# Sums of weight blocks formed at other places, and copies out of PSUM banks at a higher priority, in a one-layer encoder kernel

## The chip, the cores and the metric

The kernel runs on one core of a Trainium2 chip. The metric is device time in microseconds (us) of one execution. Three runs of the kernel before took 856.43 to 857.36 us, with a median of 857.22 us.

## The reference

One encoder layer works on 512 tokens of width 1024, in float32:

```
x += W_out [ HGRN2_group(n) ; mLSTM_group(n) ],  n = RMSNorm(x)
x += CrossAttn(RMSNorm(x), RMSNorm(mem))          (4 heads, 256 memory tokens, output matrix w_xo 1024x1024)
x += relu(RMSNorm(x) @ w_up)^2 @ w_down           (w_up 1024x4096, w_down 4096x1024)
out = RMSNorm(x)
```

The change touches what happens from the last matrix product of the cross-attention (w_xo) through the squared-ReLU part (w_up, w_down), and the order in which some transfers are issued ahead of that.

## The kernel before, in words

**Products.** TensorE multiplies float32 as two halves. ACT writes the high half of a tile (`wh`, or `xT`, `yT`, `a` for activations), VectorE (DVE) subtracts it from the source and so gets the low half (`wl`); both stand in line 325 (`split_out`). Three matmuls (high x high, high x low, low x high) then make one product. A weight block is 512 KB: it is loaded into one of three `st` buffers by SyncE (SP), split into one of three `wh` and one of three `wl` buffers, and used.

**Stream.** Up to the cross-attention's query matrix, weights come through `weights()`, which splits a few blocks ahead and loads one more (line 245). In the same call `next_form()` may do one step on sums of blocks that are needed much later.

**Seven products.** w_xo and the squared-ReLU part are cut in 2x2 blocks and computed with seven products instead of eight, named P1 to P7, each for two halves a and b (in the code g = 0, 1) of the inner dimension or of the columns. P1, P2 and P3 use plain blocks. P5, P7, P6 and P4 use sums of blocks: P7 is two blocks, P6 is P7 plus a third, P4 is P6 plus the fourth, P5 is two. The sums are never formed by an engine: a transfer puts the first block at its place, and a transfer issued by GpSimd (POOL) that adds to what stands there brings the next one. The squared-ReLU part runs as eight stages: stage 0, 2, 4, 6 are up products (one quarter of the 4096 columns each, TensorE lines 1551 to 1553) and stage 1, 3, 5, 7 are the down products of the same quarter (lines 1279 to 1281).

- The sums for the up stages, and P7 of the down stages, are made in HBM (tiles `form_<stage>_P<n>_<g>`, written by lines 282 and 298) by a fixed list of 80 steps, from which `next_form()` takes one at a time: a start (SP copies a block), an add (POOL), or a copy of a finished sum to be built on (SP, line 298).
- The sums P5, P6 and P4 of the down stages are made in SBUF, in the two buffers `msum` (tile name `as`): `sum_base` loads the first term (SP, line 282 for P5 and line 1223 for P6, which starts from the P7 in HBM), `sum_add` adds (POOL, line 282).
- The sums for w_xo are made in SBUF by `add_block` (POOL, line 1163): `U` for P5 (in an `as` buffer) and `T3` for P7, P6 and P4 in turn (tile `gate`). T3 is split for P7, then a block is added, it is split for P6, a block is added, it is split for P4.

**Order.** From w_xo on, TensorE's order is the order in which the code is written. On the other engines a scheduler orders instructions by the order of the code and by priority (`tc.high_priority()` moves an instruction ahead), and `behind(a, b)` pins a behind b on the same engine. SP and POOL issue their transfers in that order too: an issue that has to wait holds back all issues behind it on its queue. `mahead(n)` splits the weights of jobs n to n+2 of the squared-ReLU part, at high priority, and loads those of n+3 to n+6; the list `due` holds sum steps that are to be done when a job is split.

**The norm ahead of the squared-ReLU part.** While w_xo's last products are added to the residual (line 1363), `rstd_half` computes the scale of 256 tokens at a time; its last operation is a power on POOL (line 1412), one for each half of the tokens. TensorE turns the result (line 1428), ACT copies it (line 1430), and DVE multiplies the activations by it (line 1417). The residual itself is turned by TensorE (line 1389) and copied out by ACT (line 1396).

**Banks in an up stage.** P1, P6, P7 and P4 of one half accumulate in the same PSUM bank, and so do P5 and P3. After P1, P5 and P6 ACT copies the bank's present value out (lines 1557, 1564, 1567), and after P2 and P7 DVE adds it (lines 1559, 1575); the next product in that bank may start only then. In a down stage DVE adds each bank to the residual (line 1482).

Of the kernel before, what the change touches and what calls it, by code (L numbers as in the profile page):

```python
# [13 lines left out]
AF = mybir.ActivationFunctionType  # L14
ALU = mybir.AluOpType
# [3 lines left out]
P = 128  # L19
# [61 lines left out]
def trunk(ctx: ExitStack, tc: tile.TileContext, x, mem, wpk, vec, cst, lmask, rmask, rows, out):  # L81
    nc = tc.nc
# [50 lines left out]
    nh = misc[:, 0:1]  # L133
# [8 lines left out]
    def behind(a, b):  # L142

        tc.add_manual_dep(a.ins, b.ins.name, mybir.DependencyInfo(mybir.DependencyClass.NoSync, mybir.DependencyReason.DATA),
                          reason="order of an engine")
# [113 lines left out]
    def weights(key):  # L259
        i = SIDX[key]  # L260
        with (tc.high_priority() if i > 2 else ExitStack()):
            for n in range(i, i + 3):
                split(n)
            load(i + 3)
        if i >= 6 and (i < 46 or i % 3):
            next_form()
        return hl_tiles[i]

# [9 lines left out]
    def mfill(eng, dst, st, g, b, accumulate=False):  # L278
        kw = dict(accum_op=ALU.add) if accumulate else {}
        if st % 2 == 0:  # L280
            dst = dst.rearrange("p (n c) -> p n c", n=2)
        return eng.dma_start(out=dst, in_=mblock(st, g, *b), max_dma_last_dim=4096, **kw)  # L282
# [877 lines left out]

    def add_block(dst, idx, accumulate=True):
        kw = dict(accum_op=ALU.add) if accumulate else {}
        return gp.dma_start(out=dst, in_=wpk[idx], **kw)

    PLAIN = {"P1": (0, 0), "P2": (1, 0), "P3": (1, 1)}
    SUMS = {"P6": "T3", "P5": "U", "P7": "T3", "P4": "T3"}
# [50 lines left out]
    def sum_base(st, p, g):  # L1217
        t = msum[p != "P5"][:, g * 1024:g * 1024 + 1024]
        if p == "P5":
            mfill(nc.sync, t, st, g, (0, 1))  # L1220
        else:
            assert (st, "P7", g) in formed
            nc.sync.dma_start(out=t, in_=mforms[st, "P7", g][:, :], max_dma_last_dim=4096)

    def sum_add(st, p, g):
        mfill(gp, msum[p != "P5"][:, g * 1024:g * 1024 + 1024], st, g, (1, 0) if p == "P4" else (0, 0), True)

    def msplit(n):
        if n >= len(MJ):
# [18 lines left out]
    def mahead(n):  # L1248
        with tc.high_priority():
            for m in range(n, n + 3):  # L1250
                msplit(m)
            for m in range(n + 3, n + 7):
                mload(m)
        if n % 2:
            next_form()
        return mhl[n]

# [6 lines left out]
    def by_blocks(st, sta, banks, done, ready=None, after=None):  # L1264

        mlp = st >= 0
        user = {"P1": 0, "P2": 1, "P5": 2, "P6": 0, "P3": 2, "P7": 0 if mlp else 3, "P4": 0}
        opens = {"P1", "P2", "P5"} if mlp else {"P1", "P2", "P5", "P7"}
        jobs = MORDER[st] if mlp else JOBS
        held = {}  # L1270

        def product(p, g, u, w, first, end):
            for k in range(2):
                ah, al = [t[:, u * P:u * P + P] for t in sta[2 * g + k][p]]
                bh, bl = [t[:, k * 512:k * 512 + 512] for t in w]
                new = first and k == 0 and p in opens
                fl = dict(skip_group_check=True)
                ps = held[user[p]][u]
                pe.matmul(ps, lhsT=ah, rhs=bh, start=new, stop=False, **fl)  # L1279
                pe.matmul(ps, lhsT=ah, rhs=bl, start=False, stop=False, **fl)  # L1280
                pe.matmul(ps, lhsT=al, rhs=bh, start=False, stop=end and k == 1, **fl)  # L1281
            if after is not None:
                after()

        def ahead(n):
            if mlp:
                return mahead(len(JOBS) * st + n)
            with tc.high_priority():
                for m in range(n, n + 3):
                    job(m)  # L1290
                i = max(hl_tiles)
                for m in range(i + 1, i + 4):
                    load(m)
                for m in range(n + 3 - len(JOBS), n + 7 - len(JOBS)):
                    if m >= 0:
                        mload(m)
            return job(n)

        def finished(p, u):
            for t0, c, sign in INTO[mlp][p]:  # L1300
                done(t0 + u, c, held[user[p]][u], sign, (p, t0, c) in LAST[mlp])

        n = 0
        while n < len(jobs):
            p, g = jobs[n]
            if ready is not None:
                ready(p, g)
            if user[p] not in held:
                held[user[p]] = banks[user[p]]()
            if p == "P4":  # L1310
                ws = [ahead(n), ahead(n + 1)]
                for u in range(2):
                    for g in range(2):
                        product(p, g, u, ws[g], False, g == 1)
                    finished(p, u)
                n += 2
                continue
            w = ahead(n)
            for u in range(2):
                product(p, g, u, w, g == 0, g == 1)  # L1320
                if g == 1:
                    finished(p, u)
            n += 1
# [80 lines left out]
    def rstd_half(u):  # L1404

        s2_, m2_ = tiny(2), tiny(2)
        a = ap(st2, 4 * u, [2, 2], [1, 1])
        b = ap(st2, 4 * u + 1, [2, 2], [1, 1])
        v.tensor_tensor(out=s2_[:, :].unsqueeze(2), in0=a, in1=b, op=ALU.add)
        v.tensor_scalar(out=m2_, in0=s2_, scalar1=1.0 / D, scalar2=EPS, op0=ALU.mult, op1=ALU.add)  # L1410
        rt[u] = tiny(2)
        gp.tensor_tensor(out=rt[u], in0=m2_, in1=nh.to_broadcast([P, 2]), op=ALU.pow)

    def times_r(x, u, h):
        z = x[:, h * 512:h * 512 + 512]
# [42 lines left out]
        xf[p] = [YT1()[:, :], YT1()[:, :]]  # L1458
    rrow = RG()
    by_blocks(-1, sta_o, (mm2, mm2, sm2, sm2), add_out, heads_in, after_product)  # L1460
    msum.extend([A16(), A16()])
    for fn in (sum_base, sum_add):
        for q in ("P5", "P6"):
            for g in range(2):
                fn(1, q, g)


    def finish(t, r, first):
# [10 lines left out]

    def add_to(t, c, ps, sign, fin=False):  # L1480
        z = xr[t, c]
        added = v.tensor_tensor(out=z, in0=z, in1=ps, op=ALU.add if sign > 0 else ALU.subtract)  # L1482
        if not fin:
            return
        squared = stats(st3, t, c)
# [18 lines left out]
    def up(st):  # L1504
# [30 lines left out]
        for n, (p, g) in enumerate(MORDER[st]):  # L1535
# [18 lines left out]
                after_product()  # L1554
            if p == "P1":
                y[0, g] = msum[g][:, 2048:2560]
                sc.activation(y[0, g], ps, AF.Copy)
            elif p == "P2":
                v.tensor_tensor(out=y[0, g], in0=y[0, g], in1=ps, op=ALU.add)
                square(y[0, g], y[0, g])  # L1560
                form("P1", g, y[0, g], yt)
            elif p == "P5":
                y[3, g] = T2()[:, 0:512]
                sc.activation(y[3, g], ps, AF.Copy)
            elif p == "P6":
                y[1, g] = rrow[:, (1 - g) * 512:(1 - g) * 512 + 512]
                sc.activation(y[1, g], ps, AF.Copy)  # L1567
            if p in ("P3", "P6") and {("P3", g), ("P6", g)} <= set(MORDER[st][:n + 1]):
                z = y[1, g]
                v.tensor_tensor(out=z, in0=C[g], in1=z, op=ALU.subtract)  # L1570
# [132 lines left out]
```

## Time and profile before

| | us |
|---|---|
| median of three runs | 857.22 |
| profiled execution | 855.08 |
| its span (first to last instruction) | 853.2 |
| TensorE (PE) busy | 812.7 (95%) |
| VectorE (DVE) busy | 620.8 (73%) |
| ScalarE (ACT) busy | 487.3 (57%) |
| GpSimd (POOL) busy | 92.7 (11%) |

In the rows below, times count from the start of the span. A row of the timeline has the start, the duration, the engine, the line, the operation and its tiles; in brackets stands how long the engine had been idle before it and what ended that. A row of windows has the stretch and its length, the busy time and the number of instructions of each engine, then the clock granted to TensorE (1.00 is full), the busy share of the 16 DMA engines and the GB/s.

### The profile page before, as it was taken

The page shows a single profiled execution, that of the slowest core. Times are in us where ns is not written, and L with a number is a line of the kernel's source. Part 1 is how long each engine was busy: PE and PEld are TensorE (multiplying, and loading weights), DVE is VectorE, ACT ScalarE, POOL GpSimd, SP SyncE. Part 2 cuts the span into 40 slices and gives each one's busy share as a digit, 9 for nine tenths or more (in the row PEclk, how much of TensorE's full clock was granted, in tenths as well). Part 3 has the DMA queues.
Part 4 walks back from the last instruction along what each step waited for, and adds up shares of the span by engine and source line. Part 5 has one row for each costly group of instructions (what it writes and reads, how often), then busy time and mean ns, then how long its engine had stood idle before and what let it go on. Part 6 is the DMA issues. An engine that isn't in the chain of part 4 may idle for free.

```text
span 853.2 us, 14086 instructions
## 1 busy us (share of the span) xinstructions
PE 812.7 (95%) x5438; PEld 700.4 (82%) x5438; DVE 620.8 (73%) x1033; ACT 487.3 (57%) x854; POOL 92.7 (11%) x132
## 2 busy tenths in 40 slices
PE   8999999999999999999999867899899999999995
PEld 6787888877889888888888757888898799889984
DVE  6568875897589887545578577797479658865885
ACT  5247465436585575444555474763577358537854
POOL 2002000220111200100201112010202000100001
PEclk9999999999999999999999988999999999999998
DMA  7377734494469586744826939679989975876552
GB/s 270 112 243 182 219 130 148 103 233 144 150 152 263 147 279 225 188 157 129 201 67 151 238 82 265 187 191 340 260 276 244 287 222 193 205 226 215 172 148 99
DMA packets 56021, 165.16 MB, mean 194 GB/s; under 512 B 5329, under 2 KB 5457, under 8 KB 55954
## 3 DMA queue, kind: packets, MB, share of 16 engines
q1 hardware_dynamic: 40624, 123.94, 41.7%
q0 software_dynamic: 15040, 39.85, 25.4%
q8 instruction: 43, 0.70, 0.3%
q10 hardware_dynamic: 290, 0.47, 0.2%
q14 instruction: 24, 0.20, 0.1%
HBM read 162.14 MB, written 44.04 MB: 242 GB/s over the span
## 4 chain that ended last, share of the span: by engine, by line
PE 55%; DVE 13%; DMA 12%; issue 9%; ACT 8%; POOL 1%; POOLq 0%; ACTq 0%; SPq 0%; DVEq 0%
PE mm L328 9%; PE mm L330 9%; PE mm L329 9%; DMA st<-in_wpk 6%; DVE wl L325 6%; ACT wh L325 5%; PE sm L1281 3%; PE sm L1280 3%; PE sm L1279 3%; DMA st<-form_P 3%; PE sm L1551 2%; PE sm L1552 2%; PE sm L1553 2%; DMA gate<-in_wpk 2%; PE mm L1552 1%
## 5 line engine op out<-in xcount | busy, mean ns | idle before, releaser
L325 ACT ACTIVATE wh<-st 128x1024 fp32r<-128x1024 f32 x163 | 172.3, 1059 | 188.0 <-PE mm L329 43.6
L325 DVE TENSOR_TENSOR wl<-st,wh 128x1024 fp32r<-128x1024 f32 x163 | 199.0, 1223 | 109.5 <-ACT wh L325 108.1
L328 PE MATMUL mm<-xT,wh 128*128 128x512 f32 x288 | 115.5, 402 | 0.0
L330 PE MATMUL mm<-xT,wl 128*128 128x512 f32 x288 | 113.1, 393 | 0.1
L329 PE MATMUL mm<-xT,wh 128*128 128x512 f32 x288 | 112.7, 391 | 0.3 <-DVE xT L1042 0.3
L1279 PE MATMUL sm<-wh,a 128*128 128x512 f32 x180 | 70.3, 390 | 1.2 <-DVE vv L1482 1.2
L1281 PE MATMUL sm<-wh,a 128*128 128x512 f32 x180 | 70.3, 391 | 0.9 <-DVE a L325 0.9
L1280 PE MATMUL sm<-wl,a 128*128 128x512 f32 x180 | 70.3, 391 | 0.5 <-DVE wl L325 0.5
L330 PEld LDWEIGHTS mm<-xT,wl 128*128 128x128 f32 x288 | 54.1, 188 | 11.7 <-DVE wl L325 0.3
L329 PEld LDWEIGHTS mm<-xT,wh 128*128 128x128 f32 x288 | 54.2, 188 | 10.9 <-DVE xT L1042 0.9
L328 PEld LDWEIGHTS mm<-xT,wh 128*128 128x128 f32 x288 | 54.1, 188 | 10.8 <-ACT wh L325 0.3
L282 POOL DMA_DIRECT2D form_P<-in_wpk x40 | 42.7, 1508 | 68.9 <-DMA form_P<-form_P 53.1
L282 POOL DMA_DIRECT2D as<-in_wpk x24 | 21.2, 894 | 240.9 <-DMA as<-in_wpk 97.4
L1551 PE MATMUL sm<-yT,wh 128*128 128x256 f32 x128 | 38.5, 301 | 6.6 <-ACT rg L1567 6.6
L1281 PEld LDWEIGHTS sm<-wh,a 128*128 128x128 f32 x180 | 33.8, 188 | 8.6 <-DVE a L325 1.6
L1279 PEld LDWEIGHTS sm<-wh,a 128*128 128x128 f32 x180 | 33.8, 188 | 8.5 <-ACT wh L325 1.6
L1280 PEld LDWEIGHTS sm<-wl,a 128*128 128x128 f32 x180 | 33.8, 188 | 8.3 <-DVE wl L325 1.4
L325 ACT ACTIVATE wh<-as 128x1024 fp32r<-128x1024 f32 x26 | 27.5, 1056 | 19.3 <-PE sm L1281 13.3
L1552 PE MATMUL sm<-yT,wh 128*128 128x256 f32 x128 | 38.0, 297 | 0.0
L1553 PE MATMUL sm<-yT,wl 128*128 128x256 f32 x128 | 37.9, 296 | 0.0
L1552 PE MATMUL sm<-xT,wh 128*128 128x256 f32 x128 | 36.3, 284 | 1.0 <-DVE xT L325 1.0
L1553 PE MATMUL mm<-xT,wl 128*128 128x256 f32 x128 | 36.3, 284 | 0.7 <-DVE wl L325 0.7
(388 smaller groups left out, 2134.7 us busy)
## 6 DMA issues: line engine op xcount, KB each, us to landing
st<-in_wpk SPq DMA_DIRECT2D x123, 512.0 KB, 4.2
form_P<-in_wpk POOLq DMA_DIRECT2D x40, 512.0 KB, 10.2
st<-form_P SPq DMA_DIRECT2D x40, 512.0 KB, 6.2
as<-in_wpk POOLq DMA_DIRECT2D x28, 512.0 KB, 8.3
form_P<-in_wpk SPq DMA_DIRECT2D x24, 512.0 KB, 6.2
form_P<-form_P SPq DMA_DIRECT2D x16, 512.0 KB, 5.9
gate<-in_wpk POOLq DMA_DIRECT2D x8, 512.0 KB, 6.1
as<-in_wpk SPq DMA_DIRECT2D x8, 512.0 KB, 3.6
```

What stands on the lines that cost most here:

```text
L282: return eng.dma_start(out=dst, in_=mblock(st, g, *b), max_dma_last_dim=4096, **kw)
L325: return sc.activation(dst_hi, src, AF.Copy), v.tensor_tensor(out=dst_lo, in0=src, in1=dst_hi.bitcast(F32), op=ALU.subtract)
L328: pe.matmul(ps, lhsT=ah, rhs=bh, start=first, stop=False)
L329: pe.matmul(ps, lhsT=ah, rhs=bl, start=False, stop=False)
L330: pe.matmul(ps, lhsT=al, rhs=bh, start=False, stop=last)
L1279: pe.matmul(ps, lhsT=ah, rhs=bh, start=new, stop=False, **fl)
L1280: pe.matmul(ps, lhsT=ah, rhs=bl, start=False, stop=False, **fl)
L1281: pe.matmul(ps, lhsT=al, rhs=bh, start=False, stop=end and k == 1, **fl)
L1551: pe.matmul(o, lhsT=hi[:, z], rhs=xh[:, m], start=new, stop=False, **fl)
L1552: pe.matmul(o, lhsT=hi[:, z], rhs=xl[:, m], start=False, stop=False, **fl)
L1553: pe.matmul(o, lhsT=lo[:, z], rhs=xh[:, m], start=False, stop=kt == 3, **fl)
```

## The change

```diff
@@ weights(key)
-        if i >= 6 and (i < 46 or i % 3):
+        if i >= 6:
             next_form()
@@ add_block
-        return gp.dma_start(out=dst, in_=wpk[idx], **kw)
+        pool_add[0] = gp.dma_start(out=dst, in_=wpk[idx], **kw)
@@ sum_base(st, p, g)
         if p == "P5":
-            mfill(nc.sync, t, st, g, (0, 1))
+            o = mfill(nc.sync, t, st, g, (0, 1))
         else:
-            nc.sync.dma_start(out=t, in_=mforms[st, "P7", g][:, :], max_dma_last_dim=4096)
+            o = nc.sync.dma_start(out=t, in_=mforms[st, "P7", g][:, :], max_dma_last_dim=4096)
+        behind(o, last_load[0])
@@ sum_add(st, p, g)
-        mfill(gp, msum[p != "P5"][:, g * 1024:g * 1024 + 1024], st, g, (1, 0) if p == "P4" else (0, 0), True)
+        o = mfill(gp, msum[p != "P5"][:, g * 1024:g * 1024 + 1024], st, g, (1, 0) if p == "P4" else (0, 0), True)
+        behind(o, last_made[0] if st > 1 or p != "P5" else pool_add[0])
@@ mahead(n)
-        if n % 2:
+        if n % 2 and n >= len(JOBS):
             next_form()
@@ by_blocks, ahead(n)  (w_xo)
+            if n == 4:
+                msum.append(A16())
+                for g in range(2):
+                    sum_base(1, "P5", g)
             return job(n)
@@ rstd_half
-        gp.tensor_tensor(out=rt[u], in0=m2_, in1=nh.to_broadcast([P, 2]), op=ALU.pow)
+        pool_add[0] = gp.tensor_tensor(out=rt[u], in0=m2_, in1=nh.to_broadcast([P, 2]), op=ALU.pow)
@@ behind w_xo
-    msum.extend([A16(), A16()])
-    for fn in (sum_base, sum_add):
-        for q in ("P5", "P6"):
-            for g in range(2):
-                fn(1, q, g)
+    msum.append(A16())
+    due.extend((2 + g, sum_add, 1, "P5", g) for g in range(2))
+    due.extend((3 + 2 * g, sum_base, 1, "P6", g) for g in range(2))
+    due.extend((7 + 2 * g, sum_add, 1, "P6", g) for g in range(2))
@@ add_to (down stages)
-        added = v.tensor_tensor(out=z, in0=z, in1=ps, op=ALU.add if sign > 0 else ALU.subtract)
+        with tc.high_priority():
+            added = v.tensor_tensor(out=z, in0=z, in1=ps, op=ALU.add if sign > 0 else ALU.subtract)
@@ up(st): the copies behind P1, P5 and P6 (ACT) and the add behind P2 (DVE), each in the same way
-                sc.activation(y[1, g], ps, AF.Copy)
+                with tc.high_priority():
+                    sc.activation(y[1, g], ps, AF.Copy)
```

TensorE's order is the same in both kernels. Below, the rows of the other engines' orders are given at three places; the second number in a tile's name counts tiles and differs between the kernels without meaning.

**POOL, from w_xo's last sums to the first down stage.** `gate` is T3, `as` are the sums of the first down stage, the two TENSOR_TENSOR are the norm's powers, `form` are the sums in HBM. Before:

```order
L1163 DMA gate_631_4282<-in_wpk 128x1024
L282 DMA as_791_5101<-in_wpk 128x1024 x2
L1163 DMA gate_630_4281<-in_wpk 128x1024
L282 DMA as_792_5102<-in_wpk 128x1024 x2
L1163 DMA gate_631_4282<-in_wpk 128x1024
L1412 TENSOR_TENSOR tiny_773_5014<-tiny_772_5011,misc_75 128x2
L1412 TENSOR_TENSOR tiny_790_5099<-tiny_789_5096,misc_75 128x2
L282 DMA form_6_P7_1_3344<-in_wpk 256x1x512
L282 DMA form_4_P5_0_3327<-in_wpk 256x1x512
L282 DMA form_7_P7_0_3337<-in_wpk 128x1024
L282 DMA form_6_P5_0_3339<-in_wpk 256x1x512
L282 DMA form_4_P5_1_3331<-in_wpk 256x1x512
```

With the change (line 1420 is the power):

```order
L1163 DMA gate_631_4288<-in_wpk 128x1024
L1163 DMA gate_630_4287<-in_wpk 128x1024
L1163 DMA gate_631_4288<-in_wpk 128x1024
L1420 TENSOR_TENSOR tiny_774_5024<-tiny_773_5021,misc_75 128x2
L1420 TENSOR_TENSOR tiny_791_5109<-tiny_790_5106,misc_75 128x2
L282 DMA as_739_4829<-in_wpk 128x1024 x2
L282 DMA as_792_5111<-in_wpk 128x1024 x2
L282 DMA form_6_P5_1_3343<-in_wpk 256x1x512
L282 DMA as_792_5111<-in_wpk 128x1024 x2
```

The four adds to `as` have moved from between T3's adds to behind the second power, and six adds to `form` that stood behind it (five are shown) are gone from here: they now stand ahead of T3's adds, in the stream.

**SP, in the stream, where the first extra steps fall.** `st` are weights, `vv` the residual, `form` a start. Before:

```order
L245 DMA st_482_3425<-in_wpk 128x1024
L245 DMA st_496_3477<-in_wpk 128x1024
L282 DMA form_6_P7_0_3340<-in_wpk 256x1x512
L245 DMA st_505_3521<-in_wpk 128x1024
L282 DMA form_4_P7_1_3332<-in_wpk 256x1x512
L245 DMA st_514_3565<-in_wpk 128x1024
```

With the change:

```order
L245 DMA st_482_3425<-in_wpk 128x1024
L282 DMA form_6_P7_0_3340<-in_wpk 256x1x512
L245 DMA st_496_3478<-in_wpk 128x1024
L282 DMA form_4_P7_1_3332<-in_wpk 256x1x512
L245 DMA st_505_3522<-in_wpk 128x1024
L282 DMA form_5_P7_1_3336<-in_wpk 128x1024
L245 DMA st_514_3566<-in_wpk 128x1024
```

Each start has moved up by a place or more; none moves below a load that it stood ahead of.

**ACT, in the first up stage, around the copies behind P6.** `wh` is a split of weights, `rg` the copy of P6's bank. Before (line 1567 is the copy, the first for a, the second for b):

```order
L1567 ACTIVATE rg_700_4634<-sm_796_5117 128x512
L1511 ACTIVATE as_791_5101<-as_791_5101 128x512
L325 ACTIVATE yT_804_5215<-as_791_5101 128x512
L325 ACTIVATE wh_834_5454<-st_821_5325 128x1024
L1510 ACTIVATE as_792_5102<-as_792_5102 128x512
L1510 ACTIVATE rg_700_4634<-rg_700_4634 128x512
L1511 ACTIVATE as_792_5102<-as_792_5102 128x512
L1511 ACTIVATE rg_700_4634<-rg_700_4634 128x512
L325 ACTIVATE wh_838_5491<-st_826_5359 128x1024
L325 ACTIVATE yT_813_5285<-as_792_5102 128x512
L325 ACTIVATE gate_830_5420<-rg_700_4634 128x512
L1567 ACTIVATE rg_700_4634<-sm_808_5224 128x512
```

With the change (line 1579 is the copy):

```order
L1579 ACTIVATE rg_700_4641<-sm_796_5119 128x512
L325 ACTIVATE xT_693_4632<-a4_770_5012 128x1024
L325 ACTIVATE yT_813_5288<-as_792_5111 128x512
L325 ACTIVATE wh_834_5457<-st_821_5329 128x1024
L1579 ACTIVATE rg_700_4641<-sm_808_5227 128x512
```

Ten instructions stood between the two copies, now three do.

More of the change, by code (lines that the diff above doesn't have):

```diff
@@ L1162, in add_block @@
         kw = dict(accum_op=ALU.add) if accumulate else {}
-        return gp.dma_start(out=dst, in_=wpk[idx], **kw)
+        pool_add[0] = gp.dma_start(out=dst, in_=wpk[idx], **kw)
+    pool_add = [None]
     PLAIN = {"P1": (0, 0), "P2": (1, 0), "P3": (1, 1)}
@@ L1556, in up @@
                 y[0, g] = msum[g][:, 2048:2560]
-                sc.activation(y[0, g], ps, AF.Copy)
+                with tc.high_priority():
+                    sc.activation(y[0, g], ps, AF.Copy)
             elif p == "P2":
-                v.tensor_tensor(out=y[0, g], in0=y[0, g], in1=ps, op=ALU.add)
+                with tc.high_priority():
+                    v.tensor_tensor(out=y[0, g], in0=y[0, g], in1=ps, op=ALU.add)
                 square(y[0, g], y[0, g])
@@ L1563, in up @@
                 y[3, g] = T2()[:, 0:512]
-                sc.activation(y[3, g], ps, AF.Copy)
+                with tc.high_priority():
+                    sc.activation(y[3, g], ps, AF.Copy)
             elif p == "P6":
                 y[1, g] = rrow[:, (1 - g) * 512:(1 - g) * 512 + 512]
-                sc.activation(y[1, g], ps, AF.Copy)
+                with tc.high_priority():
+                    sc.activation(y[1, g], ps, AF.Copy)
             if p in ("P3", "P6") and {("P3", g), ("P6", g)} <= set(MORDER[st][:n + 1]):
```

## The prediction, made before the change was run

> **What bounds the kernel now.** I read the page first, then TensorE's share by windows, and then the rows of its timeline at each dip.
>
> ```profile
> PE 812.7 (95%) x5438; PEld 700.4 (82%) x5438; DVE 620.8 (73%) x1033; ACT 487.3 (57%) x854; POOL 92.7 (11%) x132
> ...
> 340.00:460.00 120.00, 119.73 (x600) 99.78 (x600) 72.47 (x147) 61.27 (x134) 12.12 (x14) 1.00 0.56 148
> 500.00:560.00 60.00, 49.73 (x363) 47.68 (x362) 47.50 (x59) 41.03 (x63) 7.75 (x8) 0.91 0.72 195
> ...
> 485.00:490.00 5.00, 3.28 (x19) 1.00 1.06 243
> 495.00:500.00 5.00, 4.64 (x18) 0.60 0.36 102
> ...
> 520.00:525.00 5.00, 4.33 (x37) 1.00 1.07 280
> 525.00:530.00 5.00, 0.94 (x2) 0.63 1.09 301
> 530.00:535.00 5.00, 5.00 (x32) 0.69 1.08 303
> 535.00:540.00 5.00, 5.00 (x44) 1.00 1.07 266
> 540.00:545.00 5.00, 2.80 (x24) 1.00 0.78 265
> 545.00:550.00 5.00, 4.17 (x23) 0.68 0.40 135
> ...
> 610.00:615.00 5.00, 3.02 (x26) 1.00 1.09 280
> 615.00:620.00 5.00, 4.37 (x20) 0.50 1.10 269
> ```
>
> TensorE is busy 95%, so only its 40 us of gaps, and what a lowered clock costs behind them, can be won by new orders. The two longer windows show all engines in turn (PE, PEld, DVE, ACT, POOL): the stream from 340 to 460 us has no gap, 119.73 of 120 us. The short windows show TensorE alone: the dips are at 488, 525, 543 and 613 us, and behind each the granted clock is 0.50 to 0.69, so that "busy" there is slow work: 32 matmuls in 5 us instead of 44.
>
> ```profile
> 483.13 0.39 PE L1279 MATMUL sm<-wh,a 128*128 128x512 f32 x1
> 485.85 1.03 PE L1389 MATMUL sm<-cs,vv 128*128 128x128 f32 x8
> 486.64 0.48 PE L1279 MATMUL mm<-wh,yT 128*128 128x512 f32 x1
> 487.88 0.40 PE L1281 MATMUL mm<-wh,yT 128*128 128x512 f32 x1
> 495.23 2.35 PE L1389 MATMUL sm<-cs,vv 128*128 128x128 f32 x8 [6.96 <-DVE vv L1363]
> 499.51 0.39 PE L1428 MATMUL sm<-cs,tiny 128*128 128x128 f32 x2
> 502.86 0.36 PE L1551 MATMUL sm<-xT,wh 128*128 128x256 f32 x1
> 527.89 0.58 PE L1551 MATMUL mm<-yT,wh 128*128 128x256 f32 x1 [3.56 <-ACT t L1564]
> 529.64 0.58 PE L1552 MATMUL mm<-yT,wh 128*128 128x256 f32 x1 [1.17 <-DVE yT L325]
> 545.83 0.39 PE L1551 MATMUL sm<-yT,wh 128*128 128x256 f32 x1 [3.02 <-ACT rg L1567]
> 558.92 0.40 PE L1279 MATMUL sm<-wh,yT 128*128 128x512 f32 x1
> ...
> 763.73 0.28 PE L1551 MATMUL sm<-xT,wh 128*128 128x256 f32 x1
> ...
> 804.92 0.40 PE L1279 MATMUL sm<-wh,yT 128*128 128x512 f32 x1
> ```
>
> The first up stage takes from 502.86 to 558.92, 56.1 us; the last takes from 763.73 to 804.92, 41.2 us. The first also holds turns of the residual and the norm's scale, about 1 us, so it loses 13.9 us.
>
> **First wait: T3's last add.** At 487.9 us TensorE stands in w_xo's P4. Who holds it is read from POOL, ACT and DVE:
>
> ```profile
> 467.49 1.83 POOL L282 DMA_DIRECT2D as<-in_wpk  x2 [15.37 <-PE mm L1281]
> 473.48 1.22 DVE L325 TENSOR_TENSOR wl<-gate,wh 128x1024 fp32r<-128x1024 f32 x1
> 478.54 0.88 POOL L282 DMA_DIRECT2D as<-in_wpk  x1 [2.91 <-DMA as<-form_P]
> 479.08 13.08 DMA gate<-in_wpk
> 483.01 0.62 ACT L1022 ACTIVATE t<-vv 128x512 f32<-128x512 f32 x1
> 492.27 1.06 ACT L325 ACTIVATE wh<-gate 128x1024 fp32r<-128x1024 f32 x1 [8.55 <-DMA gate<-in_wpk]
> 493.35 1.23 DVE L325 TENSOR_TENSOR wl<-gate,wh 128x1024 fp32r<-128x1024 f32 x1 [9.00 <-ACT wh L325]
> ```
>
> T3's second half was free for its last add at 473.48 + 1.22 = 474.7, but POOL stood in front of two adds to the down stage's sums, one of them waiting for its first term (as<-form_P). So the add was issued at 479.08, and it took 13.08 us (the chain of waits) beside four adds and two first terms of the same sums. The split of P4's weights waited 8.55 us for it, DVE's residual additions (L1363) stand behind that split, and TensorE's turns behind them.
>
> The change takes all four adds out from between, and P6's first terms too. The add is issued at about 474.9. Such an add lands in 6.1 us by the page's median for `gate`; the split cannot start before 483.7 anyway, since ACT is in its residual squares until then (483.01 and its read-out) and one of three buffers comes free only when TensorE leaves P3's first half at 483.13. So the split moves from 492.27 to 483.7, if the add lands within 8.8 us, and the residual additions, the squares, the power, its turn and the first scaled activations follow as before. From 487.88 to 499.51 are 11.6 us; undisturbed they are 0.4 + 0.8 for the turns (485.85 to 486.64) + 1.5 for six matmuls, so 9.0 us are lost. ACT's copies of the turned residual now become the latest, by about 0.8 us: **8.2 us** won. Bounds: 1 (the add lands as late as before, only issued earlier by 4 us beside other loads) to 9.
>
> The lowered clock is part of it: the eight turns took 2.35 us at 495.23, 1.03 at 485.85. The Trainium skill ("TensorE: Matmul & The Clock Gate", "HAM oscillation — how this bites in real kernels") says that gaps above about 3.4 us drop the clock to half; by it, only the gaps of 6.96 and 3.56 would cost clock. The windows speak otherwise: behind the gap of 3.02 us at 545.83 the clock is 0.68 and 23 matmuls ran where 44 do. By the skill's rule the sum below would be about 1.5 us smaller; the rows decide.
>
> **Second: the first up stage.** Here two edits meet: seven steps leave it, and copies out of banks come earlier.
>
> ```profile
> 509.42 5.20 POOL L282 DMA_DIRECT2D form_P<-in_wpk  x5
> 522.73 1.06 ACT L325 ACTIVATE wh<-st 128x1024 fp32r<-128x1024 f32 x1 [5.52 <-DMA st<-in_wpk]
> ...
> q1 hardware_dynamic: 40624, 123.94, 41.7%
> q0 software_dynamic: 15040, 39.85, 25.4%
> ...
> form_P<-in_wpk POOLq DMA_DIRECT2D x40, 512.0 KB, 10.2
> ...
> as<-in_wpk POOLq DMA_DIRECT2D x28, 512.0 KB, 8.3
> ...
> gate<-in_wpk POOLq DMA_DIRECT2D x8, 512.0 KB, 6.1
> ```
>
> Five adds are issued at once behind the second power; ACT then waits 5.52 us for a load of weights, at the head of its queue, with the copy of P5's bank (L1564) behind it: that is TensorE's wait of 3.56. The wait of 3.02 at 545.83 has no transfer in it: the copy of P6's bank stood behind ten other ACT instructions, now three. In matmuls: 520 to 535 us have 71 instead of 132, 6.9 us lost; 540 to 550 have 47 of 88, 4.7 us. Together 11.6; the remaining 2.3 of the 13.9 stand at the stage's begin, in the norm's own chain, and stay.
>
> What a step costs: POOL's 76 transfers take 25.4% of 853.2 us, 2.85 us of all 16 engines each; one of SP's 512 KB takes 41.7% x 853.2 x 0.524 / 123.94 = 1.5 us. Out go six adds and a start, 18.6 us; in come four adds and two first terms, 14.4 us. That is little less in sum, but no five at once: two adds behind the power, two when the first terms have landed, one step (form_6_P5_1) behind these. Each load of weights has about 7 us from issue to need, and I expect most to land in it.
>
> What is late next is DVE: busy 47.5 of the 60 us, idle 12.5. All the 11.6 would leave it full, so I take three quarters: **8.5 us**. Bounds: 0 (transfers as late as before) to 12.
>
> **Third: later stages.** The dip at 613 us (46 of 88 matmuls, 4.8 us) has a load that waits beside adds, too; the same transfers remain, but two of three adds that were issued together now go ahead of the down stage's sums. I take **1.5** (0 to 4.8). The bank copies and the residual additions at higher priority meet short waits of 0.4 to 1.2 us in the last stages: **0.8** (-1 to 2).
>
> **The seven steps in the stream.** Their 18.6 us of transfers now lie between 340 and 460 us, where the DMA engines are 0.56 busy (53 of 120 us free) and TensorE never waits. This cover hides them; were a load late by all of one add, it would cost 2.85 us. I take **-0.3** (0 to -3). The new pins (`behind`) add no wait of their own: behind the adds that now stand behind the power, only a later step and adds of the down stage are queued on POOL, and the down stage's sums are split some 45 us later. SP's two moved first terms wait for a buffer that P5's split has left long before.
>
> **Sum.** 8.2 + 8.5 + 1.5 + 0.8 - 0.3 = 18.7 us. The profiled execution took 855.08, which would become 836.4; it lies 2.1 us below the median of the runs, so the prediction is 838.5. A measurement of this kernel can tell about 0.2%, 1.7 us, from no change.
>
> **Rivals.**
> - *T3's add stays late.* Its 13.08 us may come less from the sums' transfers than from the loads of weights, which remain. Then the first term gives 1 instead of 8.2: 845.7. For it: the DMA share is above 1 at 480 to 490 us; against it: most of what filled that stretch leaves it. Chance 0.12.
> - *The transfers in the first up stage stay late.* 14.4 us come for 18.6, in a shorter stage. A load then waits as at 522.73, and the earlier copies only wait at the head of the queue: the second term gives 3, the third 0: 845.5. The Trainium skill ("DMA: Bandwidth & Descriptors", "Queues, rings and completion order") says that each engine takes turns between the queues that have work; by that, two queued adds slow a load as much as five do while they last, which is this rival's mechanism. The trace shows loads of 10 us beside five adds, none beside two. Chance 0.16.
> - *Slower: copies hold the splits back.* A copy at the head of ACT or DVE waits for TensorE's product; if the split behind it is for the very next product, TensorE waits for 1.06 + 1.23 = 2.3 us. There are eight such copies and additions in each of four up stages. From nine of the 32 on (20.7 us) the change loses more than it wins by over 0.2%; twelve would give 866. Against it: a split of job n+2 needs the `wh` buffer that job n-1 leaves, which is the product that the copy waits for. Chance 0.05.
> - *It doesn't do what it says.* The orders show that the steps did move, so this has no chance of its own; one add of the list still runs in the first up stage.
>
> **How the numbers follow.** The forecast has 0.62. Both first rivals together (0.02) give 853; for no change within 0.2% I leave 0.03, where T3's gain is given back. So faster 0.92, same 0.03, slower 0.05. The range goes from all terms near their upper bounds (9 + 12 + 4.8 + 2, 829) to a little beyond either of the first two rivals (850).
>
> **What would show it.** T3's last add issued near 475 us and no gap of TensorE near 488: the first term. No wait of TensorE above 1 us for the copies of lines 1564 and 1567 in the first up stage, and DVE above 90% busy in it: the second. A first up stage of 47 us with the clock at 1.00; if it still takes 54, the second rival. Loads in the stream that hold TensorE between 340 and 460 us, or gaps in the later up stages with ACT or DVE waiting for TensorE in front of a split, would make the prediction wrong.

## The result and the profile after

The changed kernel takes **848.46 us** (median of 5 runs, 846.51 to 850.25) against 857.06 us (5 runs, 854.22 to 857.36) for the kernel before: a ratio of 0.9906 with a 95% interval of 0.9879 to 0.9932. It is faster by 8.6 us; 18.7 us were forecast. The profiled execution took 848.46 us, its span is 846.6 us.

The first matmul of each stage on TensorE, from the timeline of the changed kernel (start, duration, engine, line; lines 1559 to 1561 are up products, 1283 to 1285 down products):

```profile
492.97 0.36 PE L1559 MATMUL sm<-xT,wh 128*128 128x256 f32 x1
...
539.84 0.40 PE L1283 MATMUL sm<-wh,yT 128*128 128x512 f32 x1
...
627.63 0.40 PE L1283 MATMUL sm<-wh,yT 128*128 128x512 f32 x1
...
716.58 0.40 PE L1283 MATMUL sm<-wh,yT 128*128 128x512 f32 x1
...
798.57 0.40 PE L1283 MATMUL sm<-wh,yT 128*128 128x512 f32 x1
```

Such starts, read in the same way in every trace, give the lengths of the stages (us). The last column is the end of TensorE's last matmul.

| | w_xo ends | up 0 | down 1 | up 2 | down 3 | up 4 | down 5 | up 6 | down 7 | end |
|---|---|---|---|---|---|---|---|---|---|---|
| before | 502.9 | 56.1 | 39.6 | 45.9 | 38.9 | 42.1 | 38.3 | 41.2 | 39.8 | 844.7 |
| after | 493.0 | 46.9 | 45.6 | 42.1 | 45.1 | 43.8 | 38.1 | 43.9 | 39.4 | 838.0 |
| won (+) | 9.9 | 9.2 | -6.0 | 3.8 | -6.2 | -1.7 | 0.2 | -2.7 | 0.4 | 6.7 |

Up to 540 us the forecast's two large terms came: 9.9 for 8.2, and 9.2 for 8.5. From there on four stages are longer than before. The rows of the changed kernel that answer to those of before, first TensorE's waits and its windows:

```profile
528.22 0.39 PE L1559 MATMUL sm<-yT,wh 128*128 128x256 f32 x1 [0.39 <-ACT rg L1579]
554.11 0.79 PE L1283 MATMUL sm<-wh,a 128*128 128x512 f32 x1 [5.92 <-ACT a L325]
604.46 0.39 PE L1559 MATMUL mm<-yT,wh 128*128 128x256 f32 x1 [1.55 <-ACT t L1575]
654.27 0.50 PE L1283 MATMUL sm<-wh,a 128*128 128x512 f32 x1 [1.15 <-ACT wh L325]
...
691.96 0.39 PE L1559 MATMUL mm<-yT,wh 128*128 128x256 f32 x1 [1.74 <-ACT t L1575]
773.93 0.39 PE L1559 MATMUL mm<-yT,wh 128*128 128x256 f32 x1 [1.82 <-ACT t L1575]
```

```profile
340.00:460.00 120.00, 119.73 (x601) 99.82 (x600) 72.49 (x147) 60.75 (x134) 17.23 (x19) 1.00 0.67 169
493.00:540.00 47.00, 43.94 (x345) 42.94 (x344) 40.94 (x50) 34.88 (x54) 5.27 (x6) 0.96 0.80 225
485.00:490.00 5.00, 5.00 (x33) 4.29 (x32) 2.88 (x6) 4.63 (x12) 0.71 (x1) 1.00 0.16 48
...
545.00:550.00 5.00, 3.19 (x15) 2.30 (x13) 5.00 (x8) 4.34 (x6) 0.00 (x0) 1.00 0.34 105
550.00:555.00 5.00, 0.89 (x2) 0.67 (x3) 4.27 (x7) 0.63 (x1) 2.66 (x3) 0.51 0.53 86
```

The waits of 6.96, 3.56 and 3.02 us are gone, and the stream has no gap, at a DMA share of 0.67. A new wait of 5.92 us stands in the first down stage, with the clock at 0.51 behind it, and short ones in later stages. T3's last add is in order, by POOL's timeline and ACT's:

```profile
474.28 0.88 POOL L1163 DMA_DIRECT2D gate<-in_wpk  x1 [2.47 <-DVE wl L325]
488.14 0.71 POOL L1420 TENSOR_TENSOR tiny<-tiny,misc 128x2 f32<-128x2 f32 x1 [12.98 <-DVE tiny L1418]
```

```profile
482.65 1.06 ACT L325 ACTIVATE wh<-gate 128x1024 fp32r<-128x1024 f32 x1 [0.48 <-ACT t L1022]
```

It is issued at 474.28 and lands 5.4 us later (13.08 before); the split of its sum stands at 482.65 and waits only for the squares ahead of it on ACT.

**The first down stage.** TensorE waits there for the second half of P5's activations. This is the changed kernel's DVE and ACT up to that point, from the timeline (line 1527 subtracts for P5, 1531, 1539 and 1535 for P6, P7 and P3, 1490 adds to the residual, 325 splits):

```profile
544.82 0.63 ACT L1519 ACTIVATE t<-t 128x512 f32<-128x512 f32 x1
```

```profile
545.10 0.68 DVE L1539 TENSOR_TENSOR as<-as,t 128x512 f32<-128x512 f32 x1
545.70 0.68 DVE L1535 TENSOR_TENSOR rg<-rg,t 128x512 f32<-128x512 f32 x1
...
546.91 0.68 DVE L1490 TENSOR_TENSOR vv<-vv,sm 128x512 f32<-128x512 f32 x1
547.50 1.22 DVE L325 TENSOR_TENSOR wl<-as,wh 128x1024 fp32r<-128x1024 f32 x1
...
550.37 0.68 DVE L325 TENSOR_TENSOR a<-as,a 128x512 fp32r<-128x512 f32 x1
550.98 0.68 DVE L325 TENSOR_TENSOR a<-rg,a 128x512 fp32r<-128x512 f32 x1
551.58 1.22 DVE L325 TENSOR_TENSOR wl<-as,wh 128x1024 fp32r<-128x1024 f32 x1
552.71 0.68 DVE L1527 TENSOR_TENSOR t<-t,t 128x512 f32<-128x512 f32 x1
```

The square it needs is ready at 545.4, but the subtraction runs at 552.71, behind ten instructions, among them passes and splits for products that come after it. DVE has no gap. Either it has too much work, or the work stands in the wrong order; the rows cannot tell which.

**The second down stage** (down 3) waits for weights. SP's timeline, POOL's and ACT's:

```profile
643.41 0.33 SPq L1215 DMA_DIRECT2D st<-form_P  x1
643.79 1.38 SPq L282 DMA_DIRECT2D as<-in_wpk  x1
645.75 19.27 SPq L282 DMA_DIRECT2D st<-in_wpk  x5
```

```profile
656.24 0.87 POOL L282 DMA_DIRECT2D as<-in_wpk  x1 [12.58 <-DMA as<-in_wpk]
```

```profile
658.51 1.06 ACT L325 ACTIVATE wh<-st 128x1024 fp32r<-128x1024 f32 x1 [4.29 <-DMA st<-in_wpk]
662.30 1.06 ACT L325 ACTIVATE wh<-st 128x1024 fp32r<-128x1024 f32 x1 [2.73 <-DMA st<-in_wpk]
```

The first term of P5's next sum (as<-in_wpk) is pinned behind the last load (st<-form_P); that load had to wait 10.0 us for a buffer that DVE's split leaves, so the term goes out at 643.79, just ahead of five loads, and its add at 656.24 runs beside them.

**Up 4 and up 6** wait for a load too. In up 4, by ACT's timeline (line 1575 copies P5's bank, and TensorE's wait of 1.74 us ends with that copy):

```profile
690.36 1.06 ACT L325 ACTIVATE wh<-st 128x1024 fp32r<-128x1024 f32 x1 [4.19 <-DMA st<-form_P]
691.33 0.58 ACT L1575 ACTIVATE t<-mm 128x512 f32<-128x512 f32 x1
```

The copy stands behind a split whose weights are late.

### The profile page after: what moved, and what is told of

The parts are those of the page before. It is cut to its first block, busy times and chain, and to the rows that moved or that the text cites. A ratio compares the mean times of both kernels' runs of the same rounds, so it can differ in the third digit from the quotient of the medians.

```text
span 846.6 us, 14075 instructions
## 1 busy us (share of the span) xinstructions
PE 812.1 (96%) x5438; PEld 699.7 (83%) x5438; DVE 620.3 (73%) x1033; ACT 488.1 (58%) x854; POOL 92.4 (11%) x132
## 3 DMA queue, kind: packets, MB, share of 16 engines
q1 hardware_dynamic: 40624, 123.94, 42.1%
## 4 chain that ended last, share of the span: by engine, by line
PE 61%; DMA 12%; DVE 11%; issue 7%; ACT 6%; POOL 1%; POOLq 0%; ACTq 0%; SPq 0%; DVEq 0%
PE mm L328 10%; PE mm L330 10%; PE mm L329 9%; DMA st<-form_P 5%; DVE wl L325 5%; PE sm L1283 4%; PE sm L1284 4%; PE sm L1285 4%; DMA st<-in_wpk 4%; ACT wh L325 3%; PE mm L1559 1%; PE mm L1560 1%; PE mm L1561 1%; PE sm L1559 1%; PE sm L1561 1%
## 5 line engine op out<-in xcount | busy, mean ns | idle before, releaser
L1283 PE MATMUL sm<-wh,a 128*128 128x512 f32 x180 | 71.8, 399 | 7.9 <-ACT a L325 5.9
L1285 PE MATMUL sm<-wh,a 128*128 128x512 f32 x180 | 71.3, 396 | 0.5 <-DVE a L325 0.5
L1560 PE MATMUL sm<-xT,wh 128*128 128x256 f32 x128 | 37.1, 290 | 1.3 <-DVE xT L325 1.2
L1559 PE MATMUL sm<-xT,wh 128*128 128x256 f32 x128 | 37.4, 292 | 0.4 <-ACT xT L325 0.4
L1561 PE MATMUL sm<-xT,wl 128*128 128x256 f32 x128 | 36.9, 288 | 0.0
L1559 PE MATMUL sm<-yT,wh 128*128 128x256 f32 x128 | 36.3, 284 | 0.4 <-ACT rg L1579 0.4
L1559 PE MATMUL mm<-xT,wh 128*128 128x256 f32 x128 | 36.6, 286 | 0.0
```

Source lines behind the costliest of these rows:

```text
L1559: pe.matmul(o, lhsT=hi[:, z], rhs=xh[:, m], start=new, stop=False, **fl)
L1560: pe.matmul(o, lhsT=hi[:, z], rhs=xl[:, m], start=False, stop=False, **fl)
L1561: pe.matmul(o, lhsT=lo[:, z], rhs=xh[:, m], start=False, stop=kt == 3, **fl)
```

## The experiments

Fifteen runs follow, of thirteen kernels (k2 is j4 again, k3 is g4 again). Stage lengths are those of one profiled execution of each. Ratios are to the kernel before, in the same rounds; its median in the four sets was 856.28, 856.99, 855.75 and 856.36 us. Line numbers shift by a few between kernels.

### Which part gives time back

**Priorities and pins, each alone or left out.** e1 is the changed kernel with this edit:

```diff
@@ add_to
-        with tc.high_priority():
-            added = v.tensor_tensor(...)
+        added = v.tensor_tensor(...)
```

> The changed kernel, with the residual additions of the down stages back at normal priority; all else as changed. In the changed kernel the stages take 46.9 (first up), 45.6 (first down), 42.1, 45.1 (second down), 43.8, 38.1, 43.9, 39.4 us. Order theory: in the first two down stages VectorE runs residual additions ahead of the subtraction that makes P5's second half, and of weight splits; without their priority the first down stage takes 42 us or less and the second 42 or less, and the median falls to 842 or less. Load theory: VectorE is full there because the first up stage got shorter, whatever the order; the first down stage stays at 44.5 us or more and the median within 846 to 851.

f1 is the changed kernel with this one:

```diff
@@ up(st), behind P4
-                square(y[2, g], ps)
-                first(g)
+                with tc.high_priority():
+                    square(y[2, g], ps)
+                    first(g)
```

> The changed kernel, with the square of P4's bank and the subtraction and split that make P5's form at high priority in every up stage. Order theory: TensorE's wait of 5.9 us in the first down stage falls below 1.5, the stage takes 41 us or less, the median 843.5 or less. Load theory: what is moved back (splits of the sums, residual additions) is then waited for instead; the stage stays at 44 us or more, the median at 846 or more.

e4 is the kernel before, with only the five changes of priority.

> The kernel before, with the priorities alone (bank copies in the up stages, residual additions in the down stages); sums and steps stay where they were. Order theory: the first down stage gets longer by 3 us or more (from 39.6) though the first up stage stays above 50, so the median is 853 to 858. Load theory: the down stages stay within 1 us of before; the first up stage loses only the 3.0 us wait for P6's copy and its clock (to about 52), the median is 852 to 854.

e5 is the changed kernel without the pins of the later sums:

```diff
@@ sum_base
-        behind(o, last_load[0])
+        if st == 1:
+            behind(o, last_load[0])
@@ sum_add
-        behind(o, last_made[0] if st > 1 or p != "P5" else pool_add[0])
+        if st == 1 and p != "P4":
+            behind(o, last_made[0] if p != "P5" else pool_add[0])
```

> The changed kernel, with the sums of the second down stage and later (and the P4 adds of the first) not pinned behind a load or a split, as before the change. If the pins are what makes loads of weights late in the second down stage, it takes 41 us or less (45.1 as changed), and the last two up stages 42.5 or less, the median is 843 or less. If not, these stages stay within 1.5 us and the median within 846 to 851.

| | median | ratio [95%] | up 0 | down 1 | up 2 | down 3 | up 4 | up 6 |
|---|---|---|---|---|---|---|---|---|
| after | 848.46 | 0.9906 [0.9879, 0.9932] | 46.9 | 45.6 | 42.1 | 45.1 | 43.8 | 43.9 |
| e1, additions at normal priority | 847.10 | 0.9880 [0.9840, 0.9919] | 48.5 | 43.5 | 41.5 | 46.2 | 41.8 | 42.1 |
| f1, P5's passes at high priority | 847.82 | 0.9882 [0.9841, 0.9923] | 46.8 | 44.7 | 42.5 | 47.1 | 44.4 | 42.9 |
| e4, before + priorities | 854.83 | 0.9973 [0.9950, 0.9996] | 53.0 | 42.5 | 44.1 | 39.6 | 42.9 | 42.2 |
| e5, no later pins | 843.01 | 0.9833 [0.9797, 0.9869] | 48.4 | 45.8 | 47.3 | 38.9 | 42.3 | 41.6 |

e5 is the clear one, and came as expected: without the later pins down 3 takes 38.9 us as before, up 4 and up 6 are short again, and the kernel is 5.4 us faster than the changed one by the medians (6.2 by the ratios); the two intervals do not meet. It also loses what the pins had won in up 2 (47.3 for 42.1). Neither e1 nor f1 settled down 1. e1's 43.5 us lies between the two theories; f1's stage and time came as the load theory had them, but its wait had a reason that neither theory names. It remains at 3.54 us: DVE subtracts at 545.22, but ACT's split of the result stands at 551.74 behind a split for P3. In e4 the priorities win 3.1 us in up 0 and lose some 3 in down 1, so the order theory's figures came, but for its bound of 3 us, missed by less than 0.1.

**The sums alone, and sums with steps.** g1 is e5 without any higher priority and with the seven steps where they stood before; g2 is e5 with only the priorities taken out.

> The kernel before with the new order of the first down stage's sums alone: the seven steps stand as before, nothing has a higher priority, and no later sum is pinned. Term A of the prediction (w_xo ends some 8 us earlier) must show by itself: w_xo ends at 493 to 495 us instead of 502.9, the first up stage takes 53 to 56 us as before, since its steps' adds are back and its copies are late, and the whole takes about 848 us if nothing is given back. Rival (hand-back): w_xo's gain moves the work of DVE and ACT as little as the steps do, so the down stage is longer by 2 us or more and the whole takes 851 us or more.

> Sums and moved steps, without any higher priority and without the later pins (compare with the run without the later pins, 843.0 us, which differs by the priorities alone). Theory: the steps give most of the first up stage's gain, so it takes 48 to 51 us; with the copies later, the first down stage has less left over and takes 41 to 43 us instead of 45.8; both together as long as with the priorities, and the whole takes 842 to 846 us. Rival: the priorities give that gain, the first up stage takes 53 us or more, and the whole takes 848 us or more.

Together with e5 and the changed kernel they make a ladder, one part more on each rung (gain: 1 less the ratio, of 857 us):

| | ratio [95%] | gain, us | w_xo ends | up 0 | down 1 |
|---|---|---|---|---|---|
| g1: sums | 0.9918 [0.9888, 0.9948] | 7.0 | 493.2 | 60.0 | 39.6 |
| g2: + seven steps moved | 0.9841 [0.9809, 0.9873] | 13.6 | 493.2 | 53.2 | 39.5 |
| e5: + priorities | 0.9833 [0.9797, 0.9869] | 14.3 | 492.7 | 48.4 | 45.8 |
| after: + later pins | 0.9906 [0.9879, 0.9932] | 8.1 | 493.0 | 46.9 | 45.6 |

g1 has the whole gain of w_xo, and gives 3.9 us of it back at once: its up 0 takes 60.0 us. This is longer than the 53 to 56 us expected, and not the place that the rival named; its whole time (848.90 us) came as expected. In g1 the five steps' adds are issued together at 520.82, behind the second power and the adds to the sums; the split at 536.74 waits 3.33 us for its load, a copy of P6's bank stands behind it, and TensorE waits 6.44 us for that. Moving the steps wins 6.6 us. The priorities shorten up 0 by 4.8 us, lengthen down 1 by 6.3, and leave the time as it is. g2's up 0 came as the rival had it (53.2, for 53 or more), so the steps' part in that stage was expected too large; its time (842.64 us) came as the theory had it, and down 1 even shorter (39.5, for 41 to 43).

### Which pin

g4 is e5 with the pins of P6's sums of stage 3 put back (they fall into up 2). j2 is the changed kernel with the later first terms unpinned and the adds pinned, j3 the reverse.

> All of the change, but of the pins behind loads and splits only those of the first down stage's sums and those of P6's sums that fall into the third up stage. Theory (each pin acts where its transfers fall): the third up stage takes 42 us as after the change (47.3 without any later pin), and the fourth to eighth stages stay as without pins (38.9, 42.3, 38.1, 41.6, 39.4), so the whole takes 838 to 840 us. Rival: the adds kept out of the third up stage collide with the loads of the down stage behind it, which takes 42 us or more, and the whole takes 842 us or more.

> The whole change, but the first terms of the later sums are not pinned behind the last load on the queue; the adds stay pinned. Theory (a first term pinned behind a load that waits for its buffer holds all loads behind it on that queue): the fourth stage (45.1 us after the change) takes 39 to 41 us, and the whole takes 842 to 845 us. Rival (the adds' pins hold form adds, and so form loads, on the other queue): the fourth stage stays at 44 us or more, and the whole at 847 us or more.

> The complement: the later first terms stay pinned behind the last load, the later adds are free. By the theory of the pinned first terms the fourth stage stays at 44 us or more, and the whole takes 847 us or more. By the rival of the adds' pins that stage takes 39 to 41 us, the fifth and seventh stages 42 and 41.5 us instead of 43.8 and 43.9, and the whole takes 842 to 845 us.

| | median | ratio [95%] | up 2 | down 3 | up 4 | up 6 |
|---|---|---|---|---|---|---|
| after: both pinned | 848.46 | 0.9906 [0.9879, 0.9932] | 42.1 | 45.1 | 43.8 | 43.9 |
| j3: first terms pinned | 845.47 | 0.9867 [0.9830, 0.9903] | 41.9 | 43.3 | 44.5 | 43.2 |
| j2: adds pinned | 845.12 | 0.9879 [0.9840, 0.9919] | 48.8 | 39.6 | 41.4 | 40.8 |
| e5: neither | 843.01 | 0.9833 [0.9797, 0.9869] | 47.3 | 38.9 | 42.3 | 41.6 |
| g4: only P6's in up 2 | 840.79 | 0.9820 [0.9790, 0.9850] | 44.3 | 39.1 | 42.4 | 40.3 |

By the stages it is the first terms on SP's queue: pinned, they win 5 to 7 us in up 2 and lose 4 to 6 in down 3 and 4 to 6 in up 4 and up 6 together. j2's down 3 came as the theory of the first terms had it, and its time missed by 0.1 us (845.12, for at most 845); j3 lies between the theories (43.3 and 845.47). Their whole times are alike, and their intervals overlap with those of e5 and of the changed kernel, so the whole times do not tell the two pins apart. In e1, with all pins, the waits of up 4 and up 6 stand at the same places (1.13 and 1.51 us, for 1.74 and 1.82), but the clock stays at 1.00 behind them, where the changed kernel's falls to 0.50; whether the additions' priority decides that is not shown. g4 keeps part of the good half of the trade: its up 2 takes 44.3 us, not the 42 expected, and its time missed the 838 to 840 by 0.8; that it is faster than e5 is not shown, as the intervals overlap widely. In e5's down 3 the sums are out of the way ahead of the loads, by POOL's timeline and ACT's:

```profile
642.93 3.59 POOL L282 DMA_DIRECT2D as<-in_wpk  x4 [13.35 <-DMA as<-in_wpk]
646.08 2.58 POOL L282 DMA_DIRECT2D form_P<-in_wpk  x2
672.37 0.91 POOL L282 DMA_DIRECT2D as<-in_wpk  x1 [23.70 <-DMA as<-form_P]
```

```profile
657.20 1.06 ACT L325 ACTIVATE wh<-st 128x1024 fp32r<-128x1024 f32 x1 [5.34 <-DMA st<-form_P]
659.86 1.06 ACT L325 ACTIVATE wh<-st 128x1024 fp32r<-128x1024 f32 x1 [1.60 <-DMA st<-in_wpk]
662.54 1.06 ACT L325 ACTIVATE wh<-st 128x1024 fp32r<-128x1024 f32 x1 [1.62 <-DMA st<-in_wpk]
```

No add is issued between 648.7 and 672.4, and the splits wait 1.6 us at the places where the changed kernel's wait 4.29 and 2.73; the first wait, of 5.34 us, does not reach TensorE.

### Order or too much work

h1 is g4 with the first half's passes for P6, P7 and P3 written behind those of P5's second half, in the first up stage alone:

```diff
@@ up(st), behind P4
                 first(g)
-                if g == 0:
-                    second(g)
-                    by_p7(g)
-                    by_p3(g)
+                for h in ([0] if g == 0 and st else [0] if g and not st else []):
+                    second(h)
+                    by_p7(h)
+                    by_p3(h)
```

> As the run with the pins of the third up stage alone, and in the first up stage the passes for the first halves of P6, P7 and P3 are written behind those of P5's second half, which is used before them. Order theory: the wait of 4 to 6 us for P5's second half in the first down stage shrinks to 1.5 us or less, that stage takes 41 to 42 us instead of 45.8, and the whole is 3 to 4 us below the run without this edit. Rival (DVE is full): from 537 to 554 us DVE has passes without a gap whatever their order, so the wait only moves to P6 or to a split of weights, the stage takes 44 us or more, and the whole stays within 1.5 us.

j1 is h1 with all priorities taken out, j4 h1 with the additions' alone.

> As the run with the late passes (838.8 us), with all higher priorities taken out. Theory (the priorities move a wait from the first up stage into the down stage behind it and win nothing): these two stages together take 90 to 93 us as with the priorities (91.1), the up stage longer and the down stage shorter, and the whole stays within 1.5 us of 838.8. Rival (the copies' priority wins once the passes are in the order of their use): the two stages take 94 us or more, and the whole takes 841.5 us or more.

> As the run with the late passes, with the higher priority taken from the residual's additions alone; the copies out of banks keep it. If the additions at the head of DVE hold passes and splits of the down stages back, the first down stage (43.3 us) is shorter by 1 us or more and the whole takes 835.5 to 837.5 us; if their priority decides nothing, the whole stays within 1.5 us of 838.8.

h1 took 838.82 us (0.9806 [0.9768, 0.9844]), j1 841.06 (0.9820 [0.9788, 0.9851]), j4 836.96 (0.9772 [0.9730, 0.9814]). h1's down 1 took 43.3 us, with a wait of 2.92 left, between both theories. j4 came as expected from additions that hold passes back: its down 1 takes 39.6 us, 3.7 less than h1's. So three corners of the square of the two edits were run in the same rounds (h1 is the fourth): k1 is g4 with the additions at normal priority, k2 is j4, k3 is g4.

> The run with the pins of the third up stage, its passes in the old order, and the higher priority taken from the residual's additions alone: the fourth corner of a square of two edits (late passes, additions at normal priority). If the additions alone hold back the passes for P5's second half, the first down stage takes 40 to 41 us here too, and the whole stays within 1 us of the kernel with both edits. If the late passes alone do it, that stage keeps its wait of 4 to 6 us and takes 45 us or more, and the whole stays at 840 to 841 us. If each removes one of two causes, the stage takes 42 to 44 us, and the whole 838 to 840 us.

> The kernel with both edits, 836.96 us before, on the same chip and in the same rounds as the other two: the corner that both theories expect to be fastest, 836 to 838 us, with a first down stage of 39.5 to 41 us.

> The corner with neither edit, 840.79 us before, with a first down stage of 45 to 48 us: 840 to 842 us. If it lies within 1.5 us of the corner with both edits, the two edits are not shown to be worth anything, and the wait that goes back to the down stage is only one of several that take each other's place.

| | median (range) | ratio [95%] | up 0 | down 1 | wait in down 1 |
|---|---|---|---|---|---|
| k3: neither | 840.06 (836.54 to 842.69) | 0.9815 [0.9788, 0.9842] | 47.3 | 45.3 | 5.04 |
| k1: additions normal | 837.89 (836.43 to 840.41) | 0.9800 [0.9774, 0.9826] | 47.2 | 45.5 | 3.89 |
| k2: + late passes | 836.93 (834.74 to 838.15) | 0.9777 [0.9752, 0.9802] | 47.0 | 40.5 | 0.71 |

By the stage, the late passes decide: k1 to k2 is 5.0 us in down 1, and the additions' priority alone (k3 to k1) is nothing there. Once the passes are late, the additions take part: h1, the corner with late passes alone, has 43.3 us. By the whole time the square is not settled: k1 lies within 1 us of k2, as it would if the additions alone decided, k2 is 3.1 us below k3 with intervals that still overlap by 0.0014, the steps between are smaller than the intervals, and later stages of single executions differ by 2 to 3 us. The windows from 540 us on, k3's and then k2's, which differ by both edits:

```profile
540.00:545.00 5.00, 5.00 (x28) 4.28 (x27) 4.97 (x7) 4.94 (x9) 0.00 (x0) 1.00 0.64 206
545.00:550.00 5.00, 4.22 (x19) 3.17 (x17) 5.00 (x8) 4.29 (x6) 0.90 (x1) 1.00 0.37 116
550.00:555.00 5.00, 0.74 (x2) 0.52 (x3) 4.27 (x7) 0.94 (x2) 1.99 (x3) 0.64 0.97 197
555.00:560.00 5.00, 5.00 (x17) 4.04 (x16) 4.95 (x8) 2.69 (x4) 0.63 (x1) 0.68 1.06 210
```

```profile
540.00:545.00 5.00, 5.00 (x24) 4.12 (x23) 4.96 (x8) 4.93 (x9) 0.00 (x0) 1.00 0.59 197
545.00:550.00 5.00, 5.00 (x24) 4.14 (x23) 5.00 (x7) 4.18 (x6) 0.90 (x1) 1.00 0.58 206
550.00:555.00 5.00, 3.68 (x15) 2.43 (x14) 5.00 (x8) 2.22 (x3) 2.62 (x3) 1.00 0.93 166
555.00:560.00 5.00, 4.78 (x21) 3.63 (x20) 4.78 (x8) 2.32 (x3) 0.00 (x0) 1.00 1.06 220
```

The third busy column is DVE's: full in both, 19.2 and 19.7 of 20 us. TensorE's is the first: 66 matmuls in k3, 84 in k2. The same engine, equally full, feeds TensorE or not, by which of its passes come first. The row that moved, k3's and then k2's, from DVE's timeline:

```profile
552.86 0.68 DVE L1529 TENSOR_TENSOR t<-t,t 128x512 f32<-128x512 f32 x1
```

```profile
544.80 0.68 DVE L1528 TENSOR_TENSOR t<-t,t 128x512 f32<-128x512 f32 x1
```

The copies' priority is worth something only now. j1 and j4, same rounds, differ by it alone, and by 4.1 us in the time (with intervals that overlap by 0.0026); up 0 is 54.6 and 48.3 us, down 1 38.6 and 39.6. The two stages together take 93.1 us without it and 88.0 (j4) or 87.6 (k2) with it. In the old order of the passes they take 92.7 us both without it (g2) and with it (k1, which has the pins of up 2 besides): there it moves 6 us from one stage to the other. j1's expectation, that all priorities win nothing, missed by 0.7 us (within 1.5 of 838.8 wanted, 841.06 measured).

**The best version** is k2 and j4 (the same kernel): 836.93 us, a ratio of 0.9777 [0.9752, 0.9802]; it is faster than the kernel before and the changed one, and the intervals do not meet.

## Why the prediction was right or wrong

Faster was right; the forecast of 838.5 was 10 us too low. The range (829 to 850) held the time by luck: its upper end was drawn from the first two rivals, and neither of them is what happened. The two large terms came in full, and the stages behind them gave more than half of it back, by two steps of the working that failed.

- **T3's last add (8.2 forecast): right in mechanism, a little small.** The add is issued at 474.28 as worked out, and w_xo ends 9.9 us earlier, beyond the bound of 9: 0.7 us of it stand ahead of the wait already, and behind ACT's copies, for which 0.8 us were taken off, only DVE waits, 0.35 us for the scale; TensorE does not. As a gain of the whole kernel it is 7.0 us (g1), because up 0, whose steps are still in it there, takes 3.9 us longer.
- **The first up stage (8.5 forecast): the term came, and its end was drawn in the wrong place.** The stage is 9.2 us shorter (three quarters of 11.6 would have been 8.7, not 8.5), with no wait above 0.4 us for a copy out of a bank. The step that failed is "What is late next is DVE ... I take three quarters": the working stopped at the stage's last product. What was late next was one pass of DVE's for the down stage's fourth product: TensorE waits 5.92 us for it, as it stands behind passes that are needed later, and down 1 loses 6.0 us. DVE's amount of work was not the bound, as k2 shows; in the up stage it was 40.94 of 47 us busy, 87%, not the 90% named. The two edits of this term are not alike either: the moved steps win 6.6 us (g1 to g2), the higher priorities nothing (g2 to e5), and that of the copies something only when the passes behind are in order (j1 to j4).
- **The later stages (1.5 + 0.8 forecast): wrong in sign.** Up 2 won 3.8 us, but by the pins (47.3 us without them, 45.9 before) and not by the order of adds that the term named; down 3, up 4 and up 6 lost 10.6. The step that failed is "The new pins (`behind`) add no wait of their own". It looked at the first down stage's sums and at POOL, and asked who waits for the pinned add; the pins of the later first terms on SP, behind a load that itself waits for a buffer, were not followed. They cost 5.4 us net (e5), which the bounds of 0 to -3 did not allow. The 0.8 for the priorities in the last stages is not measured by itself.
- **The stream's steps (-0.3): right.** 119.73 of 120 us busy at a DMA share of 0.67 for 0.56.
- **The rivals.** T3's add stays late: no. The transfers in the first up stage stay late: not there; they did in down 3. Copies that hold splits back: the rows of up 4 and up 6 show the reverse, a copy (line 1575) behind a split whose weights are late.
- **The clock.** The forecast took a lowered clock behind gaps of some 3 us, against the rule that the Trainium skill ("TensorE: Matmul & The Clock Gate", "HAM oscillation — how this bites in real kernels") gives, gaps above about 3.4 us. The rows below bear the shorter gaps out.

Without the later pins the change takes 843.0 us (e5). With the pins of up 2 back, the passes in the order of their use and the additions at normal priority it takes 836.9 (k2).

## What to carry to other kernels

A gain is followed past the stage in which it falls: list what the engines still owe the next stage's first products at the moment when the earlier stage now ends, in the order of their queues. A full engine is no bound as long as what it does first is not what is needed first. A pin behind another transfer's issue inherits every wait of that issue (10.0 us for a buffer in down 3), so each pin is priced at each place in the program where it acts.

## What was not expected of the hardware

The clock granted to TensorE falls behind gaps shorter than three microseconds, and the gap's length alone does not decide. Windows of the changed kernel, behind its gaps of 1.55 us (to 604.46) and of 1.74 us (to 691.96):

```profile
604.40:606.40 2.00, 1.94 (x16) 1.94 (x17) 1.37 (x2) 0.01 (x1) 0.00 (x0) 1.00 1.08 293
606.40:608.40 2.00, 2.00 (x19) 2.00 (x19) 0.62 (x1) 1.68 (x3) 0.00 (x0) 1.00 1.10 279
692.00:694.00 2.00, 2.00 (x15) 2.00 (x16) 1.30 (x3) 1.12 (x2) 0.00 (x0) 0.88 0.32 129
694.00:696.00 2.00, 2.00 (x11) 2.00 (x11) 1.38 (x2) 1.72 (x3) 0.00 (x0) 0.50 0.72 245
```

Behind 1.55 us the clock stays at 1.00; behind 1.74 us it falls to 0.50, beginning more than a microsecond after the gap's end: 26 matmuls in 4 us where 38 fit (19 in 2 us at a clock of 1.00), 1.3 us lost beside the gap's own 1.74. In j3 two gaps of 2.65 us, at the same place in up 4 and up 6, end at 691.95 and 774.53:

```profile
692.00:694.00 2.00, 2.00 (x9) 2.00 (x10) 1.88 (x3) 1.67 (x3) 0.00 (x0) 0.50 0.31 46
...
774.50:776.50 2.00, 1.97 (x16) 1.97 (x17) 2.00 (x3) 1.68 (x2) 0.00 (x0) 1.00 0.10 16
```

One halves the clock, the other leaves it at 1.00. What else decides, these runs do not show.
